# Attention scores with both products over all 128 partition rows, and a mask product in fp32r

## The chip, the cores and the metric

The kernel runs on one core of one Trainium2 chip. The metric is the device time of one execution in microseconds (us), given as the median of several executions. The engines are TensorE (PE; its weight loads stand apart as PEld), VectorE (DVE), ScalarE (ACT), GpSimd (POOL) and SyncE (SP, which issues most loads).

## The reference, cut to what matters

Two layers of a trunk work on 256 latent and 256 context tokens of width 1024. Each layer is a gated feed-forward block, three parallel token mixers, and a second feed-forward block. Mixers A and B are attention with 8 query heads of width 64 in two groups; the four heads of a group share one key and one value head. In the second layer only the latent tokens have queries.

```python
def gqa_softmax(q, k, v, mask, sink):
    kv, g = q.shape[2], q.shape[3]
    s = jnp.einsum('bqkgd,bskd->bkgqs', q, k).astype(jnp.float32) * (q.shape[-1] ** -0.5)
    if mask is not None:
        s = jnp.where(mask, s, -jnp.inf)
    ...
    o = jnp.einsum('bkgqs,bskd->bqkgd', p.astype(v.dtype), v)
```

Mixer A masks latent keys further than 128 positions away; mixer B has no mask. Mixer C is a gated linear memory, whose weights between tokens of one block are masked by the same two triangles.

## The kernel before

All tokens (512 rows, four blocks of 128; blocks 0 and 1 latent, 2 and 3 context) stay on the chip, and weights stream in. To keep fp32 accuracy with the fp32r format, every large product is taken in three parts: high times high, high times low, low times high (`mm3`, lines 194 to 196, the bulk of the work of TensorE). ACT makes the high part of a weight tile (L162), DVE or POOL the low part (L163).

A score of one head needs 64 rows of contraction. The query tile `Q[s]` of group s stacks the high part in one half of the partitions and the low part in the other (`q_cols`, L786 and L787). The key tile `K`, `[P, 3, T]` in fp32r, has at index s the key's high part of group s in both halves, and at index 2 the low parts of the two groups, each in its own half (`k_cols`, L826 to L828). So the first score product (L1012), over 128 rows, gives high times high plus low times high; the second (L1015) runs over the 64 rows of slice `hi`, and adds high times low:

```python
nc.tensor.matmul(ps[:, :nkey], Q[:, c, q], K[:, s, k0:512], start=True, stop=False)
if masked:
    nc.tensor.matmul(ps[:, 0:256], self.identr, ..., start=False, stop=False)
nc.tensor.matmul(ps[:, :nkey], Q[hi, c, q], K[hi, 2, k0:512], start=False, stop=True)
```

Latent queries see 512 keys, context queries 256. For latent queries of mixer A a product of a bf16 identity with a bf16 mask (L1014) adds the mask between the two. An attention step works on two heads: scores, row maximum on DVE (L1017), exponential on ACT (L1027), reciprocal on DVE (L1037), scaling (L1041, L1043); two steps later the transposes of the weights (L1055) and their split into parts (L189, L190), and a step after that the products with the values (L1070, L1072). There are 32 steps in the first layer (64 products of L1015) and 16 in the second (32).

A scheduler of the framework orders each engine's instructions by its own estimates, within priorities that follow the program. Between the attention steps it places other work: the query projections of mixer B and value projection of C (`tok_tasks`), and convolution projections (`conv_task`), all in `mm3`. Each engine then runs its list strictly in that order and waits on semaphores.

The masks are loaded once, by SP, in `more_consts`: `self.mask` in fp32 for mixer C (L1223), `self.maskr` and `self.identr` in bf16 for L1014.

Of the kernel before, what the change touches and what calls it, by code (L numbers as in the profile page):

```python
# [10 lines left out]
F32 = mybir.dt.float32  # L11
F32R = mybir.dt.float32r
# [6 lines left out]
P = 128  # L19
D = 1024  # L20
NK = 8
T = 512
# [44 lines left out]
class Builder:  # L67
# [40 lines left out]
    # ---------------------------------------------------------------- units  # L108
# [78 lines left out]
    # ---------------------------------------------------------------- helpers  # L187
# [17 lines left out]
    def rsqrt(self, ss, n, scale):  # L205
        """ss [P, n] sums of squares -> 1/sqrt(ss*scale + eps)"""
# [3 lines left out]
        # x is minus half the argument, which the seed's constant allows for  # L210
# [12 lines left out]
    # ---------------------------------------------------------------- setup  # L223
# [20 lines left out]
    def more_consts(self):  # L244
# [8 lines left out]
        self.mask = load("mask", [P, 2, P], a["mask"])  # L253
# [4 lines left out]
        self.identr = cp.tile([P, P], BF16, name="identr")  # L258
        nc.vector.tensor_copy(self.identr, self.ident)
        self.maskr = cp.tile([P, 3, P], BF16, name="maskr")  # L260
        for n in range(2):
            nc.vector.tensor_copy(self.maskr[:, 2 * n, :], self.mask[:, n, :])
        nc.vector.memset(self.maskr[:, 1, :], 0.0)
# [41 lines left out]
    # ---------------------------------------------------------------- adaLN  # L305
    def ada_first(self, h):
        """half h of the shift and scale of the first sub-layer"""
# [28 lines left out]
    def ada_tasks(self, l, ms):  # L336
        """blocks ms of the modulation (shift, scale, gate of each sub-layer): products on the vector engine,
        the sum over the partitions on the tensor engine while the next block's products run"""
# [73 lines left out]
    def ada_gate(self, l, k, ps):  # L412
        """the gate rows times the weight of the sub-layer and the gain of its output's norm"""
# [22 lines left out]
    # ---------------------------------------------------------------- norms  # L436
    def prenorm_stat(self, tbs, st):
        """the normalised rows of token blocks"""
# [51 lines left out]
    def post_evac(self, st, ps, tb, n, add):  # L490
        """adds a part of half n of the output of token block tb"""
        y = self.y_half(st, tb, n)
        if add:
            self.nc.vector.tensor_tensor(out=y, in0=ps, in1=y, op=ALU.add)
        else:
            self.copy(y, ps)

    def post(self, st, ps, tbs, n, add):
        """what follows a half of the columns of a sub-layer's output: its sum and, when add is final, its norm"""
# [3 lines left out]
    def closing(self, st, streams, add, keys, mm, done, turn):  # L503
        """the last products of a sub-layer's output and what follows them. keys[n] are the units of half n,
        mm(ps, tb, i, unit) adds the product of the ith; the latent tokens come first, and their chain
        of norms runs beside the products of the others"""
# [45 lines left out]
    def post_half(self, st, tbs, n, last, ds):  # L552
        """square sums and gated copy of half n of the output, which lies in Y or, if ds, in PSUM"""
# [23 lines left out]
    # ---------------------------------------------------------------- FFN  # L577
    def ffn_tasks(self, l, i, k, streams, st, pre, done, turn, halves=None, rest=None):
        """st holds the normalised input, pre(s) brings it for the later streams;
        done(s) is called when the residual of stream s is updated"""  # L580
# [5 lines left out]
        for part, nf in enumerate(FF_PARTS):  # L586
# [41 lines left out]
            def early_half(h, s, n, hs=hs):  # L628
                """half h of the contraction of unit n for the tokens of stream s"""
                def fn(units):  # L630
# [8 lines left out]
                    # one start clears the written bits of the whole bank  # L639
# [56 lines left out]
    # ---------------------------------------------------------------- mixer  # L696
    def tok_tasks(self, l, name, n, kper, tbs, ms, evac):
        """token-major projection of the columns called name, n wide"""
# [25 lines left out]
    def by_stream(self, tasks, pre):  # L724
        """one task of several, the latent tokens first"""
# [11 lines left out]
    def rope(self, dst, src, nh, tb, cos, sin, eng=None, out=None):  # L737
        """dst, src [P, nh*64] (src may be PSUM); rotates pairs of a latent token block"""
# [735 lines left out]
```

## Time and profile before

| what | value |
|---|---|
| median of 3 runs | 2339.59 us (2339.14 to 2345.08) |
| span of the profiled execution | 2339.1 us |
| PE busy | 2243.5 us, 96% |
| DVE busy | 1574.0 us, 67% |
| ACT busy | 1025.0 us, 44% |
| POOL busy | 198.7 us, 8% |
| L1015, second score product | 96 instructions |
| attention of the first layer | 494.7 us to about 690 us |
| attention of the second layer | 1835.7 us to about 1950 us |

The profiled execution has no time of its own beside its span of 2339.1 us, which agrees with the median to 0.5 us. Busy times of PE hold the drain of each product, which lies beside the next product; so the start times in a timeline tell more of PE than its busy share.

### The profile page before, as it was taken

The numbers are of one execution on the slowest core, as the hardware profiler recorded it, in microseconds if no ns is written. First come the engines' busy times: TensorE is split into PE (matmuls) and PEld (weight loads), VectorE is DVE, ScalarE is ACT, GpSimd is POOL, SyncE is SP. The second block draws the span as 40 slices with busy tenths as digits, with TensorE's granted clock in tenths as the row PEclk, the third lists the DMA queues.
The fourth block names the chain that finished last, engine by engine and source line by source line (L and its number), as shares of the span: only waits on it lengthen the run. The fifth ranks groups of instructions, "written<-read, shape, count | busy, mean of one in ns | idle before, by whom it ended". The sixth has DMA issues, their size and how long they took to land.

```text
span 2339.1 us, 30561 instructions
## 1 busy us (share of the span) xinstructions
PE 2243.5 (96%) x11666; PEld 1848.6 (79%) x11666; DVE 1574.0 (67%) x2709; ACT 1025.0 (44%) x1637; POOL 198.7 (8%) x115
## 2 busy tenths in 40 slices
PE   7999999899999999999999989999999899996998
PEld 4877777776678888888878788787878668996997
DVE  3987775788776654664444378778768677867555
ACT  3322222567887433442222253222235488754443
POOL 0000001123410000200000020000012220003001
PEclk9999999999999999999999999999999899998999
DMA  7756563411122224434343327656643103464664
GB/s 274 224 191 184 164 215 103 133 63 38 37 89 75 81 84 135 138 122 135 117 126 117 113 90 221 193 186 192 194 126 118 55 28 118 154 227 143 189 186 144
DMA packets 123523, 322.98 MB, mean 138 GB/s; under 512 B 12392, under 2 KB 25768, under 8 KB 122608
## 3 DMA queue, kind: packets, MB, share of 16 engines
q1 hardware_dynamic: 110224, 309.83, 41.8%
q10 hardware_dynamic: 13152, 11.21, 1.6%
q8 instruction: 91, 1.49, 0.3%
q14 instruction: 56, 0.46, 0.1%
HBM read 316.72 MB, written 4.28 MB: 137 GB/s over the span
## 4 chain that ended last, share of the span: by engine, by line
PE 83%; DVE 11%; ACT 4%; issue 1%; DMA 1%; POOL 0%; ACTq 0%; DVEq 0%
PE ps L194 25%; PE ps L195 25%; PE ps L196 25%; PE ps L1244 1%; PE ps L1015 1%; DVE sm L220 1%; PE ps L1055 1%; DVE lo L163 1%; PE ps L1012 1%; DVE sm L219 1%; PE ps L364 1%; PE ps L1213 1%; DVE slot L574 1%; PE ps L1070 1%; PE ps L466 1%
## 5 line engine op out<-in xcount | busy, mean ns | idle before, releaser
L162 ACT ACTIVATE hi<-raw 128x1024 fp32r<-128x1024 f32 (+1 forms) x444 | 456.0, 1031 | 769.7 <-PE ps L195 261.8
L194 PE MATMUL ps<-slot,hi 128*128 128x512 f32 (+1 forms) x2232 | 777.6, 350 | 7.1 <-ACT slot L189 4.9
L195 PE MATMUL ps<-slot,hi 128*128 128x512 f32 (+1 forms) x2232 | 775.8, 348 | 0.5 <-DVE slot L190 0.4
L196 PE MATMUL ps<-slot,lo 128*128 128x512 f32 (+1 forms) x2232 | 773.3, 347 | 0.0
L163 DVE TENSOR_TENSOR lo<-raw,hi 128x1024 fp32r<-128x1024 f32 (+2 forms) x395 | 475.1, 1205 | 287.6 <-ACT hi L162 285.6
L194 PEld LDWEIGHTS ps<-slot,hi 128*128 128x128 f32 x2232 | 419.6, 189 | 75.6 <-ACT slot L189 7.1
L196 PEld LDWEIGHTS ps<-slot,lo 128*128 128x128 f32 x2232 | 421.1, 189 | 57.5
L195 PEld LDWEIGHTS ps<-slot,hi 128*128 128x128 f32 x2232 | 421.0, 189 | 56.1 <-DVE slot L190 1.4
L194 PE MATMUL ps<-hi,slot 128*128 128x512 f32 (+2 forms) x1048 | 404.4, 386 | 3.0 <-DVE slot L828 1.9
L195 PE MATMUL ps<-lo,slot 128*128 128x512 f32 (+2 forms) x1048 | 402.0, 384 | 4.0 <-DVE lo L163 2.5
L196 PE MATMUL ps<-hi,slot 128*128 128x512 f32 (+2 forms) x1048 | 401.4, 384 | 2.9 <-DVE slot L190 2.9
L356 DVE SCALAR_TENSOR_TENSOR t<-raw,sc,t 128x1024 f32<-128x1024 f32 x224 | 280.4, 1281 | 130.8 <-DMA raw<-in_w_ada_dram 130.6
L194 PEld LDWEIGHTS ps<-hi,slot 128*128 128x128 f32 x1048 | 199.0, 190 | 49.1 <-issue 8.9
L196 PEld LDWEIGHTS ps<-hi,slot 128*128 128x128 f32 x1048 | 198.8, 190 | 44.3 <-DVE slot L190 3.1
L195 PEld LDWEIGHTS ps<-lo,slot 128*128 128x128 f32 x1048 | 199.0, 190 | 43.8 <-DVE lo L163 4.9
L163 POOL TENSOR_TENSOR lo<-raw,hi 128x1024 fp32r<-128x1024 f32 (+1 forms) x49 | 116.8, 2389 | 683.4 <-ACT hi L162 508.8
L189 ACT ACTIVATE slot<-t 128x512 fp32r<-128x512 f32 (+1 forms) x138 | 80.3, 594 | 183.4 <-DVE t L606 158.1
L563 POOL TENSOR_TENSOR slot<-slot,slot 128x512 f32<-128x512 f32 x20 | 30.3, 1524 | 1321.4 <-DMA raw<-in_w_down_dram 733.3
L606 DVE TENSOR_TENSOR t<-ps,t 128x512 f32<-128x512 f32 (+1 forms) x88 | 54.7, 622 | 87.9 <-PE ps L196 86.7
L190 DVE TENSOR_TENSOR slot<-t,slot 128x512 fp32r<-128x512 f32 (+1 forms) x138 | 88.6, 651 | 6.9 <-ACT slot L189 6.5
L1017 DVE TENSOR_REDUCE sm<-ps 128x1 f32<-128x512 f32 (+1 forms) x96 | 55.9, 593 | 13.1 <-PE ps L1015 12.6
L466 PE MATMUL ps<-ident,t 128*128 128x128 f32 x176 | 30.5, 331 | 34.4 <-DVE t L449 33.4
(194 smaller groups left out, 1911.3 us busy)
## 6 DMA issues: line engine op xcount, KB each, us to landing
raw<-in_w_gu_dram SPq DMA_DIRECT2D x176, 512.0 KB
raw<-in_w_ada_dram SPq DMA_DIRECT2D x128, 512.0 KB
raw<-in_w_down_dram SPq DMA_DIRECT2D x92, 512.0 KB
raw<-in_w_fm_dram SPq DMA_DIRECT2D x64, 512.0 KB
raw<-in_w_br_dram SPq DMA_DIRECT2D x24, 512.0 KB
raw<-in_w_out_dram SPq DMA_DIRECT2D x24, 512.0 KB
slot<-in_w_ada_dram SPq DMA_DIRECT2D x16, 512.0 KB
raw<-in_w_down_dram SPq DMA_DIRECT2D x20, 256.0 KB
```

What stands on the lines that cost most here:

```text
L162: self.nc.scalar.activation(out=hi, in_=raw, func=AF.Copy)
L163: eng.tensor_tensor(out=lo, in0=raw, in1=hi.bitcast(F32), op=ALU.subtract)
L189: self.nc.scalar.activation(out=hi, in_=src, func=AF.Copy)
L190: self.nc.vector.tensor_tensor(out=lo, in0=src, in1=hi.bitcast(F32), op=ALU.subtract)
L194: mm(out, lh, rh, start=start, stop=False, **kw)
L195: mm(out, lh, rl, start=False, stop=False, **kw)
L196: mm(out, ll, rh, start=False, stop=stop, **kw)
L356: v.scalar_tensor_tensor(out=acc, in0=units[0], scalar=c, in1=acc, op0=ALU.mult, op1=ALU.add)
L466: nc.tensor.transpose(pt[:, o:o + P], xn[b][:, c * P:(c + 1) * P], self.ident)
L563: eng.tensor_tensor(out=self.y_half(st, tb, n), in0=src[q], in1=self.Gt[tb // 2][:, n * 512:(n + 1) * 512], op=ALU.mult)
L606: nc.vector.tensor_tensor(out=hid[:, :W], in0=ps[:, :W], in1=hid[:, :W], op=ALU.mult)
L1017: v.tensor_reduce(out=mx[:, :1], in_=ps[:, :nkey], axis=AX.X, op=ALU.max)
```

## The change

The key tile grows to `[P, 4, T]`: index 2 + s now holds the low part of group s in both halves of the partitions, for which `k_cols` makes one more copy on DVE for each group (two for each mixer, four for each layer, eight in all). The second score product runs over all 128 rows; its lower-order half now multiplies the query's low part with the key's low part, a term that was left out before. The identity and the mask for L1014 are kept in fp32r, and mixer C reads the same mask tile; the fp32 mask is now loaded into a temporary tile of the rotating pool `t512`, at the same place in SP's list. All else in the diff is comments and blank lines. In the changed file the lines behind the mask load stand one number higher (L1012 is L1013, L828 is L829, the new copy is L830).

```diff
         self.anti = load("anti", [P, P], a["anti"])
-        self.mask = load("mask", [P, 2, P], a["mask"])
+        mask = self.t512([P, 2, P])
+        nc.sync.dma_start(mask, a["mask"])
...
-        self.identr = cp.tile([P, P], BF16, name="identr")
+        self.identr = cp.tile([P, P], F32R, name="identr")
...
-        self.maskr = cp.tile([P, 3, P], BF16, name="maskr")
+        self.maskr = cp.tile([P, 3, P], F32R, name="maskr")
...
-            K = self.slot([P, 3, T], F32R)
+            K = self.slot([P, 4, T], F32R)
...
-                nc.vector.tensor_tensor(out=K[a, 2, :], in0=pt[a], in1=K[a, g, :].bitcast(F32), op=ALU.subtract)
+                nc.vector.tensor_tensor(out=K[a, 2 + g, :], in0=pt[a], in1=K[a, g, :].bitcast(F32), op=ALU.subtract)
+                nc.vector.tensor_copy(K[b, 2 + g, :], K[a, 2 + g, :])
...
-            hi = slice(64 * s, 64 * s + 64)
...
-                nc.tensor.matmul(ps[:, :nkey], Q[hi, c, q], K[hi, 2, k0:512], start=False, stop=True)
+                nc.tensor.matmul(ps[:, :nkey], Q[:, c, q], K[:, 2 + s, k0:512], start=False, stop=True)
...
-                        v.tensor_tensor(out=Wt[:, n, :], in0=src, in1=self.mask[:, dr, :], op=ALU.add)
+                        v.tensor_tensor(out=Wt[:, n, :], in0=src, in1=self.maskr[:, 2 * dr, :].bitcast(F32), op=ALU.add)
```

With the diff the scheduler places some instructions elsewhere. On PE, at the first scores of the first layer, there stood before (ps are PSUM tiles, hi and lo a weight tile's parts, slot the key, query or token tiles):

```order
L194 MATMUL ps_3807<-hi_3695,slot_3112 128x512
L195 MATMUL ps_3807<-lo_3696,slot_3112 128x512
L1012 MATMUL ps_3837<-slot_3739,slot_3763 128x512
L1014 LDWEIGHTS identr
L1014 MATMUL ps_3837<-maskr,identr 128x256
L1015 MATMUL ps_3837<-slot_3739,slot_3763 128x512
```

At the same place of PE's list stands now:

```order
L195 MATMUL ps_3811<-lo_3696,slot_3112 128x512
L196 MATMUL ps_3811<-hi_3695,slot_3114 128x512
L194 MATMUL ps_3811<-hi_3695,slot_3112 128x512
L195 MATMUL ps_3811<-lo_3696,slot_3112 128x512
L1013 MATMUL ps_3841<-slot_3739,slot_3767 128x512
L1015 MATMUL ps_3841<-maskr,identr 128x256
L1016 MATMUL ps_3841<-slot_3739,slot_3767 128x512
```

Three more projection products (L196, L194, L195) stand ahead of the first score, and the separate weight load of the identity is gone from the list.

On DVE, where the second layer's keys and queries are split ahead of its first scores, there stood before (slot_14529 and slot_14541 are the keys of mixers A and B, slot_14553 and slot_14554 the queries of the two groups):

```order
L827 COPY slot_14529<-slot_14529 64x512
L828 TENSOR_TENSOR slot_14529<-ps_14530,slot_14529 64x512
L827 COPY slot_14541<-slot_14541 64x512
L828 TENSOR_TENSOR slot_14541<-ps_14542,slot_14541 64x512
L787 TENSOR_TENSOR slot_14553<-ps_14555,slot_14553 64x4x128
L787 TENSOR_TENSOR slot_14553<-ps_14564,slot_14553 64x4x128
L787 TENSOR_TENSOR slot_14554<-ps_14555,slot_14554 64x4x128
L1017 TENSOR_REDUCE sm_14579<-ps_14575 128x1
```

There stands now on DVE (keys slot_14533 and slot_14547, queries slot_14561):

```order
L828 COPY slot_14547<-slot_14547 64x512
L830 COPY slot_14533<-slot_14533 64x512
L829 TENSOR_TENSOR slot_14547<-ps_14548,slot_14547 64x512
L828 COPY slot_14533<-slot_14533 64x512
L829 TENSOR_TENSOR slot_14533<-ps_14534,slot_14533 64x512
L830 COPY slot_14547<-slot_14547 64x512
L830 COPY slot_14533<-slot_14533 64x512
L828 COPY slot_14547<-slot_14547 64x512
L829 TENSOR_TENSOR slot_14547<-ps_14548,slot_14547 64x512
L788 TENSOR_TENSOR slot_14561<-ps_14563,slot_14561 64x4x128
L830 COPY slot_14547<-slot_14547 64x512
L788 TENSOR_TENSOR slot_14561<-ps_14572,slot_14561 64x4x128
```

Three of the four new copies stand ahead of the first split of the queries (L787 before, L788 now), the fourth right behind it.

On PE, at the first scores of the second layer, there stood before:

```order
L196 MATMUL ps_14515<-hi_14451,slot_13827 128x512
L194 MATMUL ps_14522<-hi_14451,slot_13825 128x512
L195 MATMUL ps_14522<-lo_14452,slot_13825 128x512
L1012 MATMUL ps_14575<-slot_14529,slot_14553 128x512
L1014 LDWEIGHTS identr
```

There stands now on PE (hi_14455 is hi_14451 of before):

```order
L194 MATMUL ps_14526<-hi_14455,slot_13829 128x512
L195 MATMUL ps_14526<-lo_14456,slot_13829 128x512
L196 MATMUL ps_14526<-hi_14455,slot_13831 128x512
L194 MATMUL ps_14526<-hi_14455,slot_13829 128x512
L195 MATMUL ps_14526<-lo_14456,slot_13829 128x512
L196 MATMUL ps_14526<-hi_14455,slot_13831 128x512
L194 MATMUL ps_14505<-hi_14499,slot_13830 128x512
L1013 MATMUL ps_14583<-slot_14533,slot_14561 128x512
```

Five projection products that stood behind the first scores stand ahead of them now.

## Rows read from the trace of the kernel before

**Rows 1.** The profile page: TensorE's share, and the chain that ended last, by engine

```profile
PE 2243.5 (96%) x11666; PEld 1848.6 (79%) x11666; DVE 1574.0 (67%) x2709; ACT 1025.0 (44%) x1637; POOL 198.7 (8%) x115
PE 83%; DVE 11%; ACT 4%; issue 1%; DMA 1%; POOL 0%; ACTq 0%; DVEq 0%
```

**Rows 2.** Timeline of PE, unmasked scores, 512 keys: start, duration, instruction

```profile
1936.18 0.39 PE L196 MATMUL ps<-slot,lo 128*128 128x512 f32 x1
1936.41 0.40 PE L1012 MATMUL ps<-slot,slot 128*128 128x512 f32 x1
1936.74 0.49 PE L1015 MATMUL ps<-slot,slot 64*128 64x512 f32 x1
1937.16 0.51 PE L1012 MATMUL ps<-slot,slot 128*128 128x512 f32 x1
1937.59 0.50 PE L1015 MATMUL ps<-slot,slot 64*128 64x512 f32 x1
1938.02 0.33 PE L1055 MATMUL ps<-ident,t 128*128 128x128 f32 x1
```

**Rows 3.** Timeline of PE, masked scores of the first layer

```profile
496.05 0.40 PE L1012 MATMUL ps<-slot,slot 128*128 128x512 f32 x1
496.28 0.28 PE L1014 MATMUL ps<-maskr,identr 128*128 128x256 bf16 x1
496.50 0.50 PE L1015 MATMUL ps<-slot,slot 64*128 64x512 f32 x1
496.93 0.49 PE L1012 MATMUL ps<-slot,slot 128*128 128x512 f32 x1
```

**Rows 4.** Timeline of PE, scores of context queries, 256 keys

```profile
553.45 0.28 PE L1012 MATMUL ps<-slot,slot 128*128 128x256 f32 x1
553.66 0.38 PE L1015 MATMUL ps<-slot,slot 64*128 64x256 f32 x1
553.97 0.38 PE L1012 MATMUL ps<-slot,slot 128*128 128x256 f32 x1
```

**Rows 5.** Timeline of PE, masked scores of the second layer, at half clock

```profile
1848.56 0.63 PE L1012 MATMUL ps<-slot,slot 128*128 128x512 f32 x1
1848.99 0.44 PE L1014 MATMUL ps<-maskr,identr 128*128 128x256 bf16 x1
1849.36 0.79 PE L1015 MATMUL ps<-slot,slot 64*128 64x512 f32 x1
1850.08 0.80 PE L194 MATMUL ps<-hi,slot 128*128 128x512 f32 x1
1850.68 0.60 PE L195 MATMUL ps<-lo,slot 128*128 128x512 f32 x1
```

**Rows 6.** The chain that ended last, by line: 494 to 700, then 1834 to 1960

```profile
by line: PE ps L196 12.3%; PE ps L194 12.2%; PE ps L195 12.1%; PE ps L1015 6.9%; PE ps L1055 6.4%; PE ps L1012 4.9%; PE ps L1070 3.7%; PE ps L1072 3.6%; ACT t L1027 3.3%; DVE sm L1017 2.8%; DVE t L190 2.6%; DVE slot L960 2.5%; DVE sm L1024 
by line: PE ps L1015 12.0%; PE ps L194 11.9%; PE ps L196 11.5%; PE ps L195 10.9%; PE ps L1055 10.7%; PE ps L1012 9.7%; PE ps L1070 5.9%; PE ps L1072 5.3%; DVE sm L1017 2.2%; PE ps L1014 2.1%; ACT t L1027 1.8%; DVE sm L1033 1.7%; PE ps L1136 
```

**Rows 7.** Busy time by 25-us window: PE, PEld, DVE, ACT, POOL, granted clock

```profile
545.00:570.00 25.00, 22.39 (x121) 17.44 (x121) 20.01 (x71) 15.13 (x38) 10.22 (x9) 0.93 0.15 46
620.00:645.00 25.00, 23.60 (x127) 17.69 (x126) 17.22 (x39) 22.50 (x41) 11.04 (x7) 1.00 0.08 24
1885.00:1910.00 25.00, 23.26 (x136) 17.61 (x135) 21.14 (x53) 20.51 (x44) 3.18 (x3) 0.86 0.01 2
1910.00:1935.00 25.00, 25.00 (x158) 20.34 (x158) 18.93 (x48) 24.18 (x45) 13.97 (x8) 1.00 0.20 64
```

**Rows 8.** The same windows for L1015 alone: PE, PEld, clock

```profile
620.00:645.00 25.00, 4.48 (x10) 1.83 (x10) 1.00 0.08 24
1835.00:1860.00 25.00, 4.75 (x6) 1.71 (x6) 0.68 0.07 22
1910.00:1935.00 25.00, 3.95 (x8) 1.46 (x8) 1.00 0.20 64
```

**Rows 9.** Line L827, the copy of the keys' high parts: nanoseconds min/median/max

```profile
L827 DVE CAST slot<-slot x8: 421/422/2282, 485.6 to 1833.7; 64x512 fp32r<-64x512 f32 x8
```

**Rows 10.** Timeline: first scores of the second layer

```profile
1835.73 0.77 PE L1012 MATMUL ps<-slot,slot 128*128 128x512 f32 x1 [8.41 <-DVE slot L787]
```

More of the change, by code (lines that the diff above doesn't have):

```diff
@@ L257, in more_consts @@
         nc.vector.memset(self.ones, 1.0)
-        self.identr = cp.tile([P, P], BF16, name="identr")
+        self.identr = cp.tile([P, P], F32R, name="identr")
         nc.vector.tensor_copy(self.identr, self.ident)
-        self.maskr = cp.tile([P, 3, P], BF16, name="maskr")
+        self.maskr = cp.tile([P, 3, P], F32R, name="maskr")
         for n in range(2):
-            nc.vector.tensor_copy(self.maskr[:, 2 * n, :], self.mask[:, n, :])
-        nc.vector.memset(self.maskr[:, 1, :], 0.0)
+            nc.vector.tensor_copy(self.maskr[:, 2 * n, :], mask[:, n, :])
+        nc.vector.memset(self.maskr[:, 1, :].bitcast(F32), 0.0)
     def load_layer(self, name, shape, src, bufs=1):
```

## The prediction

> **What bounds the kernel now.** I read the page first, then the chain of waits, then timelines of TensorE in the two attention stages, since the change touches nothing else of weight. TensorE is busy for 96% of the span, and the chain that ended last runs on it for 83% [rows 1]: time taken out of TensorE's list counts, as long as nothing else is late. The timelines show what the busy share hides: how long one product holds up the next. Read the start times, not the durations. In a plain stream a product over 512 columns starts 0.23 us after the one before (1936.18 to 1936.41) [rows 2]. Around the half-row product L1015 the stream breaks up: L1012, ahead of it, holds the engine for 0.33 us instead of 0.23, L1015 itself for 0.42, and the L1012 behind it, which stands ahead of another L1015 as well, for 0.43 [rows 2]. So one L1015 costs 0.10 us ahead of itself, 0.19 in itself, and 0.10 behind itself: 0.39 us over a full-row product of the same columns. The other forms say the same. With 256 keys L1012 takes 0.21 and L1015 0.31 [rows 4], where 0.12 would be half of 0.23: again 0.09 and 0.19. With a mask ahead, the L1014 of 256 columns takes 0.22 instead of 0.12, and L1015 0.43 [rows 3]; the L1012 in front of L1014 keeps its 0.23, so the bf16 mask product itself disturbs nothing. At half clock, where L1012 takes 0.43, L1014 takes 0.37, L1015 0.72 and the L194 behind it 0.60 [rows 5]: 0.16 (over half of 0.43) and 0.29 and 0.17, in all 0.62.
>
> **The change part by part.**
>
> *Second product over all rows.* L1015 becomes a product of the same shape as L1012 and the streams around it, so I take the whole 0.39 us (0.62 at half clock) as gone. Six products lie in the cold stretch 1835 to 1860 [rows 8]; I price those six cold and the other 90 warm. In the first layer that is 64 x 0.39 = 25.0 us of TensorE's time, in the second 26 x 0.39 + 6 x 0.62 = 13.9, together 38.9.
>
> Not all of it lies on the path. In the window from 494 to 700, 206 us long, L1015 has 6.9% of the chain, 14.2 us [rows 6]. All 64 hold the engine for 32 x 0.42 + 32 x 0.31 = 23.4 us (half of them have 512 keys, half 256). So 61% lie on the path; the rest pass while TensorE would have waited for DVE or ACT anyway. From 1834 to 1960, 126 us, L1015 has 12.0%, 15.1 us [rows 6], of 26 x 0.42 + 6 x 0.72 = 15.2: practically all. On the path the saving is 25.0 x 0.61 + 13.9 = 29.2 us.
>
> *What is late next.* The softmax on DVE and ACT must now keep up with a faster TensorE. From 620 to 645 ACT is busy for 22.50 of 25 us [rows 7], which leaves 2.5 us, and 10 products there [rows 8] would save 3.9: 1.4 too much. From 1910 to 1935 ACT has 24.18 [rows 7], which leaves 0.8, and 8 products [rows 8] would save 3.1: 2.3 too much. That is 3.7 us that engines without idle time cannot give. Engines that run their lists in order never use all their idle time, so I double it: 7.4 us taken back, an estimate from these rows. Its bounds are 0 (lists fit as well as now) and all 29.2.
>
> *Eight more copies on DVE.* The nearest row is L827, the same copy of the high parts: 0.42 us, once 2.28 [rows 9]. The order shows three copies ahead of the first split of queries that the first score waits for, in the second layer and likewise in the first: 3 x 0.45 with the gaps = 1.35 us later. What covers it: five projection products are moved ahead of the scores in the second layer, 5 x 0.23 = 1.15 us, three in the first, 0.69 us. Loss 0.2 + 0.7 = 0.9 us. Behind the waiting score stand TensorE's whole list and the softmax; in the second layer TensorE already waits 8.41 us there [rows 10]. With a copy of 2.28 in each place the loss would be about 2 us more for each copy that is hit; without any cover 2.7 us; without any effect 0.
>
> *Mask in fp32r, mask load.* A 256-column product in fp32r is what L1012 with 256 keys is, and half of 0.23 us is what L1014 takes now without the disturbance of L1015; the separate load of the identity joins the stream. I take 0, with 32 x 0.1 = 3.2 us as the upper bound if the identity's load is not hidden. The mask's load keeps its place in SP's list, so no weight comes later. Mixer C reads another tile of the same shape and takes the same time. The added low-times-low term costs nothing: a product's columns decide its place in the stream, not its rows.
>
> *Sum.* 2339.1 - 29.2 + 7.4 + 0.9 = 2318.2 us. The profiled span is within 0.5 us of the median, so I forecast 2318.5 us.
>
> *A rule against it.* The start times say that a full-row product hides the weight load of the next one, since only 0.23 us pass between starts [rows 2]. The Trainium skill, "TensorE: Matmul & The Clock Gate", Part 3, under what overlaps and what doesn't, says that a weight load overlaps running products only when the row group differs. By that rule a product over 128 rows would hold up its neighbours as one over 64 does, and the sum would be 2339 instead of 2318; the stream of this kernel disagrees with it.
>
> **The rivals.**
>
> *Full effect, 2301 (2299 to 2309).* DVE and ACT follow: all 38.9 us, less 0.9 for the copies. For it: from 1910 to 1935 TensorE has no idle time at all though ACT is busy for 24.18 of 25 us [rows 7], so a nearly full neighbour need not stall it. Against: 39% of the first layer's saving is off the chain now.
>
> *The softmax takes it all, 2337 (2332.6 to 2339).* The waits of TensorE grow by as much as the products shrink. For it: from 545 to 570 TensorE is busy for 22.39 of 25 us, DVE for 20.01 [rows 7], so TensorE waits already where no product is slow. Against: in the second layer L1015 is almost wholly on the chain [rows 6], and there at least 13.9 - 2 x 2.3 = 9 us should show; to lose that too the lists must fit much worse.
>
> *The stall stays, 2339.* The price belongs to what the second product does, loading new weights and adding into a bank that was just written, and not to its 64 rows; then the weight load of a full-row second product is not hidden either, and 96 products stall as before. Against: `mm3` adds three products with new weights into one bank, 0.23 us apart [rows 2]. The rule of the Trainium skill above (same page, Part 3) would end here.
>
> *The clock falls more often, 2350.* TensorE waits more, and the granted clock drops to 1.2 GHz after waits. It does so now: 0.93 from 545 to 570 and 0.86 from 1885 to 1910, windows in which TensorE was idle for 2.6 and 1.7 us [rows 7], and 0.68 around the wait of 8.41 us [rows 8, 10]. A mean of 0.86 means 28% of 25 us at half clock, 7 us, which cost 3.5. The two stages have some twelve windows of 25 us; if the nine that keep the full clock fell as far, that is 32 us against the 21 saved: 2350. It decides from six such windows on. Against: from 620 to 645 TensorE idles 1.4 us and keeps 1.00 [rows 7].
>
> **How the numbers follow.** A measurement of this kernel can tell about 0.3%, 7 us, from no change: 2332.6 and 2346.6. Chances: my forecast, a partial gain from 2309 to 2332.6, 0.67; full effect 0.13; softmax takes it all 0.10; the stall stays 0.04; slower by the clock 0.06. Faster is 0.67 + 0.13 = 0.80, same 0.14, slower 0.06. The range reaches down into the full effect, to 2302, and up just into the swallowed case, to 2334; about 0.05 lie below and 0.15 to 0.2 above.
>
> **What would show it.** Right: second products start 0.23 us (0.12 with 256 keys) before their successor, and L1012 ahead of them too; L1014 in fp32r about 0.12; first scores in the second layer wait some 9 us for the query split; TensorE's waits for DVE and ACT between 494 and 700 grow by several us, and L1015's share of the chain falls under half. Wrong: starts still 0.42 apart; cold windows inside the attention stages; L1014 at 0.2 us; or differences outside the two attention stages, where I expect the same distances as before.

## The result, and the profile of the changed kernel

The changed kernel takes 2327.83 us (median of 4 runs, 2321.42 to 2328.41), the kernel before 2339.36 us in the same comparison (4 runs, 2337.81 to 2345.08). The ratio is 0.9944, with an interval from 0.9931 to 0.9956: faster by 11.5 us. The forecast was 2318.5 us with a range from 2302 to 2334. The profiled execution of the changed kernel is the fastest of its four (2321.42 us, span 2319.6), so it stands 19.5 us under the profiled span of before: more than the medians differ by, and the text below says where that comes from. One run of all those below, of e10, took 2751.70 us at a mean granted clock of 0.75 and is left out of its median. Lines stand one number higher than before: L1013 is the first product, L1015 the mask, L1016 the second product.

The page, in the form of [rows 1]:

```profile
PE 2207.9 (95%) x11666; PEld 1844.3 (80%) x11666; DVE 1572.1 (68%) x2717; ACT 1023.0 (44%) x1637; POOL 198.1 (9%) x115
PE 80%; DVE 11%; ACT 6%; issue 2%; DMA 1%; POOL 0%; ACTq 0%; DVEq 0%; POOLq 0%
```

As many matmuls as before (11666) keep TensorE busy for 35.6 us less, yet the span falls by 19.5 only; ACT's share of the chain has grown from 4% to 6%.

The timeline of PE where unmasked scores of the second layer run, which answers to [rows 2]:

```profile
1909.10 0.40 PE L1013 MATMUL ps<-slot,slot 128*128 128x512 f32 x1
1909.34 0.39 PE L1016 MATMUL ps<-slot,slot 128*128 128x512 f32 x1
1909.57 0.40 PE L1013 MATMUL ps<-slot,slot 128*128 128x512 f32 x1
1909.81 0.40 PE L1016 MATMUL ps<-slot,slot 128*128 128x512 f32 x1
1910.04 0.60 PE L1056 MATMUL ps<-ident,t 128*128 128x128 f32 x4
```

Read the start times again: 0.24, 0.23, 0.24, 0.23 us, where [rows 2] had 0.33, 0.42, 0.43, 0.43. The second product has become one more piece of the plain stream. With 256 keys it is the same (compare [rows 4]): 0.11 and 0.12 us from start to start.

```profile
553.53 0.28 PE L1013 MATMUL ps<-slot,slot 128*128 128x256 f32 x1
553.64 0.28 PE L1016 MATMUL ps<-slot,slot 128*128 128x256 f32 x1
553.76 0.28 PE L1013 MATMUL ps<-slot,slot 128*128 128x256 f32 x1
```

The first scores of the second layer, the place of [rows 10], and masked scores a little later:

```profile
1830.80 0.76 PE L1013 MATMUL ps<-slot,slot 128*128 128x512 f32 x1 [8.35 <-DVE slot L788]
1831.36 0.41 PE L1015 MATMUL ps<-maskr,identr 128*128 128x256 f32 x1
1831.58 0.63 PE L1016 MATMUL ps<-slot,slot 128*128 128x512 f32 x1
1832.00 0.63 PE L1013 MATMUL ps<-slot,slot 128*128 128x512 f32 x1
...
1834.89 0.39 PE L194 MATMUL ps<-hi,slot 128*128 128x512 f32 x1
1835.12 0.39 PE L195 MATMUL ps<-lo,slot 128*128 128x512 f32 x1
1835.35 0.39 PE L196 MATMUL ps<-hi,slot 128*128 128x512 f32 x1
1835.58 0.40 PE L1013 MATMUL ps<-slot,slot 128*128 128x512 f32 x1
1835.82 0.28 PE L1015 MATMUL ps<-maskr,identr 128*128 128x256 f32 x1
1835.93 0.39 PE L1016 MATMUL ps<-slot,slot 128*128 128x512 f32 x1
1836.16 0.39 PE L194 MATMUL ps<-hi,slot 128*128 128x512 f32 x1
```

The wait for the query split is still there, 8.35 us. The fp32r mask takes 0.11 us at full clock. The engine starts at half clock (0.42 us for the second product), and is back at full clock 4 us later, while [rows 5] still shows half clock 13 us behind the first score.

To see where the time went, one view of each kernel: busy time in the two attention stages, each from its first score to its last (PE, PEld, DVE, ACT, POOL, then the granted clock, DMA share and GB/s). The kernel before:

```profile
494.70:675.30 180.60, 172.90 (x877) 127.08 (x877) 141.90 (x367) 135.37 (x291) 55.70 (x36) 0.99 0.14 43
1835.70:1937.20 101.50, 96.54 (x512) 69.78 (x512) 72.90 (x178) 73.66 (x149) 25.17 (x13) 0.89 0.10 32
```

The changed kernel:

```profile
495.10:669.00 173.90, 154.87 (x876) 125.47 (x875) 140.25 (x367) 134.32 (x293) 55.90 (x36) 0.98 0.14 44
1830.80:1918.20 87.40, 79.08 (x506) 66.75 (x507) 69.58 (x179) 72.34 (x148) 25.18 (x13) 0.98 0.11 37
```

Three things are to be read here. TensorE's busy time falls by 18.0 us in the first layer and by 17.5 in the second. Its idle time (length less busy) grows from 7.7 to 19.0 us and from 5.0 to 8.3: 14.6 us together. And the granted clock of the second layer rises from 0.89 to 0.98: of 101.5 us some 11.2 were lost to half clock (0.11 x 101.5), now 1.7 of 87.4; in the first layer it goes the other way, 1.8 to 3.5. The same arithmetic gives each stage a length at full clock, its length times its clock: 178.8 and 90.3 us before, 170.4 and 85.7 after. It is an estimate, since it takes TensorE for the limit wherever the clock was halved. Outside the two stages the kernels take 2057.0 and 2058.3 us, nearly the same, as the prediction expected.

What TensorE waits for in the first layer's attention of the changed kernel (487 to 693, the four longest rows; line that waits, what it waits for, us in total, times, longest):

```profile
PE ps L1071 <- ACT t L1028: 4.5, 2, 3.4
PE ps L1056 <- ACT t L1028: 2.6, 4, 0.8
PE ps L194 <- DVE slot L829: 2.6, 1, 2.6
PE ps L1071 <- ACT t L189: 2.1, 2, 1.9
```

L1071 is a product with the values, L1056 the transpose of the weights, L1028 the exponential on ACT. The two rows that end with L1028 have 7.1 us, where the longest rows of before were 2.3 us (L1055 for DVE's L1020), 1.4 and 1.1. (The 2.6 us of L194 for L829 stand ahead of the first score, and were 1.9 before.) By the program neither product reads the exponential that ended its wait: L1071 multiplies the split weights of an earlier step, L1056 reads weights that were scaled after their exponential. Both write into one of the kernel's eight PSUM tiles, and an exponential, once it has read its scores, frees one; that they wait for the tile is read from the program, since the trace does not name it.

The longest of these waits can be followed back. The chain that ended last (the first three lines), then the timeline:

```profile
524.92 1.35 DVE slot L1144 x4
526.27 1.11 DVE slot L1146
528.17 1.21 DVE slot L1155
530.89 0.20 DVE L1021 TENSOR_SCALAR sm<-sm,nsink 128x1 f32<-128x1 f32 x1
531.12 0.69 ACT L1028 ACTIVATE t<-ps,sm 128x512 f32<-128x512 f32 x1 [3.31 <-DVE sm L1021]
531.96 0.58 PE L1071 MATMUL ps<-t,slot 128*128 128x256 f32 x1 [3.40 <-ACT t L1028]
```

ACT had been idle for 3.31 us as well. What both waited for is VectorE: between the row maximum (L1018, at 524.33) and its scaling (L1021) its list holds the scans and gates of mixer C, lines 1144 to 1155, for 6 us. The kernel before has the same scans at the same place and reaches the same product 37.1 us behind its first score, the changed kernel 36.9, with the longer wait:

```profile
525.42 1.74 DVE slot L1143 x4
531.84 0.39 PE L1070 MATMUL ps<-t,slot 128*128 128x256 f32 x1 [0.71 <-ACT t L1027]
```

So nearly all that the first layer's products had saved up to 532 us was lost again at this one place: a wait of 3.40 us (3.38 in e1 and in e3) instead of 0.71, 2.7 of the 11.3 us by which the first layer's idle time grew. Behind that wait, from 530.90 to 537.70, the granted clock is 0.50, which by the estimate above costs another 3.4 us.

In the second layer, a stretch of the changed kernel in the form of [rows 7]:

```profile
1890.00:1915.00 25.00, 24.08 (x176) 21.87 (x175) 20.18 (x52) 24.84 (x47) 14.94 (x8) 1.00 0.17 55
```

ACT is busy for 24.84 of 25 us and TensorE, for 24.08, almost as much: two full engines.

### The profile page after: what moved, and what is told of

Its sections match the earlier page's. It is cut to its first block, busy times and chain, and to the rows that moved or that the text cites. A ratio compares the mean times of both kernels' runs of the same rounds, so it can differ in the third digit from the quotient of the medians.

```text
span 2319.6 us, 30573 instructions
## 1 busy us (share of the span) xinstructions
PE 2207.9 (95%) x11666; PEld 1844.3 (80%) x11666; DVE 1572.1 (68%) x2717; ACT 1023.0 (44%) x1637; POOL 198.1 (9%) x115
## 4 chain that ended last, share of the span: by engine, by line
PE 80%; DVE 11%; ACT 6%; issue 2%; DMA 1%; POOL 0%; ACTq 0%; DVEq 0%; POOLq 0%
PE ps L194 25%; PE ps L195 24%; PE ps L196 24%; PE ps L1245 1%; DVE sm L220 1%; ACT t L1028 1%; DVE lo L163 1%; ACT hi L162 1%; DVE slot L575 1%; PE ps L365 1%; DVE sm L219 1%; PE ps L1214 1%; PE ps L467 1%; DMA slot<-in_w_ada_dram 1%; ACT t L1042 1%
## 5 line engine op out<-in xcount | busy, mean ns | idle before, releaser
L194 PE MATMUL ps<-slot,hi 128*128 128x512 f32 (+1 forms) x2232 | 777.8, 350 | 6.6 <-ACT slot L189 4.9
L195 PE MATMUL ps<-slot,hi 128*128 128x512 f32 (+1 forms) x2232 | 775.5, 348 | 0.5 <-DVE slot L190 0.3
L196 PE MATMUL ps<-slot,lo 128*128 128x512 f32 (+1 forms) x2232 | 773.1, 347 | 0.0
L194 PEld LDWEIGHTS ps<-slot,hi 128*128 128x128 f32 x2232 | 419.4, 189 | 75.3 <-ACT slot L189 6.2
L196 PEld LDWEIGHTS ps<-slot,lo 128*128 128x128 f32 x2232 | 420.6, 189 | 57.8
L195 PEld LDWEIGHTS ps<-slot,hi 128*128 128x128 f32 x2232 | 420.5, 189 | 56.3 <-DVE slot L190 1.4
L194 PE MATMUL ps<-hi,slot 128*128 128x512 f32 (+2 forms) x1048 | 402.5, 384 | 4.1 <-DVE slot L829 2.6
L195 PE MATMUL ps<-lo,slot 128*128 128x512 f32 (+2 forms) x1048 | 400.5, 382 | 4.1 <-DVE lo L163 4.1
L196 PE MATMUL ps<-hi,slot 128*128 128x512 f32 (+2 forms) x1048 | 400.4, 383 | 2.9 <-DVE slot L190 2.9
L194 PEld LDWEIGHTS ps<-hi,slot 128*128 128x128 f32 x1048 | 198.7, 190 | 48.7 <-issue 8.1
L195 PEld LDWEIGHTS ps<-lo,slot 128*128 128x128 f32 x1048 | 198.5, 189 | 43.1 <-DVE lo L163 5.0
L196 PEld LDWEIGHTS ps<-hi,slot 128*128 128x128 f32 x1048 | 198.2, 189 | 42.9 <-DVE slot L190 3.2
L190 DVE TENSOR_TENSOR slot<-t,slot 128x512 fp32r<-128x512 f32 (+1 forms) x138 | 88.7, 652 | 5.8 <-ACT slot L189 5.3
L1018 DVE TENSOR_REDUCE sm<-ps 128x1 f32<-128x512 f32 (+1 forms) x96 | 55.2, 591 | 8.1 <-PE ps L1016 7.7
```

Of the source, the lines that this page charges most:

```text
L190: self.nc.vector.tensor_tensor(out=lo, in0=src, in1=hi.bitcast(F32), op=ALU.subtract)
L194: mm(out, lh, rh, start=start, stop=False, **kw)
L195: mm(out, lh, rl, start=False, stop=False, **kw)
L196: mm(out, ll, rh, start=False, stop=stop, **kw)
L1018: v.tensor_reduce(out=mx[:, :1], in_=ps[:, :nkey], axis=AX.X, op=ALU.max)
```

## The experiments

Each ratio is to the kernel before on the same chip, whose medians were 2340.35 us (17 runs) for e1 to e4, 2340.65 (19) for e6, e7, e9 and e10, and 2339.67 (17) for e5, e8, e11 and e12. "At full clock" is always a stage's length times its granted clock, from one profile.

**Rows alone (e1_full_rows).** Before, with the four-row key tile, the copies and the full-row product, and the mask left in bf16:

```diff
-            K = self.slot([P, 3, T], F32R)
+            K = self.slot([P, 4, T], F32R)
...
+                nc.vector.tensor_copy(K[b, 2 + g, :], K[a, 2 + g, :])
...
-                nc.tensor.matmul(ps[:, :nkey], Q[hi, c, q], K[hi, 2, k0:512], start=False, stop=True)
+                nc.tensor.matmul(ps[:, :nkey], Q[:, c, q], K[:, 2 + s, k0:512], start=False, stop=True)
```

> Second product over all rows with the eight copies, mask and identity still in bf16. Theory A (the gain comes from the second product's rows): the time of the whole change, 2322 to 2329 us; second products 0.23 us (0.12 with 256 keys) before their successor. Theory B (the gain comes from the mask product in fp32r): 2337 to 2341 us.

Measured: 2324.96 us (6 runs), ratio 0.9939 (0.9924 to 0.9953). The whole gain is here.

**Mask alone (e2_mask_fp32r).** Before, with identity and mask in fp32r and the mask loaded into a temporary tile:

```diff
-        self.identr = cp.tile([P, P], BF16, name="identr")
+        self.identr = cp.tile([P, P], F32R, name="identr")
...
-        self.maskr = cp.tile([P, 3, P], BF16, name="maskr")
+        self.maskr = cp.tile([P, 3, P], F32R, name="maskr")
```

> Mask and identity in fp32r and the mask loaded into a temporary tile, second product still over 64 rows. Theory A: no change, 2336 to 2342 us, second products still 0.42 us before their successor. Theory B: 2322 to 2329 us.

Measured: 2339.7 us (12 runs), ratio 1.0001 (0.9991 to 1.0011). The mask's type is worth nothing either way.

**The changed kernel once more (e3_after_again).** No edit; it ran on the same chip as e1, e2 and e4.

> The changed kernel once more, unedited, for a second profile. Its four runs were one of 2321.4 (the profiled one) and three near 2328. Theory C (TensorE's clock differs between runs): 2321 to 2329 us, and a profile that is longer than 2319.6 us of span has more half-clock time in the attention stages, about 12 us more for 6 us of time (say 20 us instead of 10.2 in the second layer). Theory D (waits on transfers or engines differ): the same half-clock stretches to 1 us, and 6 us more of waits elsewhere.

Measured: 2324.76 us (6 runs), ratio 0.9939 (0.9925 to 0.9953). Its profile (span 2325.4) shows how far two executions of one kernel differ:

```profile
496.50:674.90 178.40, 158.12 (x875) 128.03 (x874) 140.48 (x367) 134.27 (x293) 55.89 (x36) 0.96 0.14 43
1836.20:1923.60 87.40, 79.03 (x506) 66.70 (x507) 69.52 (x179) 72.25 (x148) 25.17 (x13) 0.98 0.12 37
```

The second layer repeats to 0.1 us. The first is 4.5 us longer than in the profile above, at a clock of 0.96 instead of 0.98; at full clock it is 171.3, as against 170.4. So a large part of the 5.8 us between the two spans is clock, and it fell in the first layer.

**Keys of mixer A ahead of the queries, those of B behind (e4_keys_a_first).** The changed kernel with the order of the preparing steps changed (`k_cols` takes one mixer at a time):

```diff
-        out += vm_[:nv] + one(self.k_cols) + qcols(0) + qb[:QC]
+        out += vm_[:nv] + one(lambda R: self.k_cols(R, 0)) + qcols(0) + one(lambda R: self.k_cols(R, 1)) + qb[:QC]
```

> The changed kernel with the program order keys of mixer A, queries of mixer A, keys of mixer B. DVE then splits the queries after two new copies and without the keys of B ahead. Theory E (the wait ahead of the second layer's first score and the half clock behind it cost 5 to 10 us): that wait falls from 8.4 to about 5 us, the half-clock stretch shrinks, 2317 to 2325 us. Theory F (the softmax is late anyway): within 2 us of the changed kernel, about 2327 us.

Measured: 2321.87 us (6 runs), ratio 0.9925 (0.991 to 0.9941), 2.9 us under e3 with intervals that overlap. The time lies in Theory E's range, but the wait of the second layer's first score only fell to 8.01 us: E's mechanism did not show.

**Without the scaling of the weights (e6_no_scale_before, e7_no_scale_after).** The same edit in both kernels:

```diff
-            for e in range(2):
-                t = E[i][e]
-                if x == 0 or e == 0:
-                    nc.scalar.activation(out=t[:, :nkey], in_=t[:, :nkey], func=AF.Copy, scale=r[:, e:e + 1])
-                else:
-                    nc.gpsimd.tensor_scalar(out=t[:, :nkey], in0=t[:, :nkey], scalar1=r[:, e:e + 1], scalar2=None,
-                                            op0=ALU.mult)
```

> The kernel before, with the scaling of the attention weights by the reciprocal of their sum left out (ACT loses 176 instructions of 0.45 to 0.65 us in the attention stages, POOL 16), so that the softmax has slack. Theory G (the softmax on ACT and DVE takes back most of the first layer's saving): the second score products stay as they are, and the gap to its partner with full rows is 20 us or more. Theory H (it is the copies and the clock): the gap is that of the unedited kernels, 12 to 17 us.

> The changed kernel with the same scaling left out. Theory G: 20 us or more under its partner, and from its first score to its last score the first layer gains 12 us or more where the unedited pair gained 6.6. Theory H: 12 to 17 us under its partner, first layer as in the unedited pair.

Measured: 2349.87 us (4 runs), ratio 1.0043 (1.0027 to 1.006), for the kernel before; 2325.78 (4), ratio 0.9943 (0.9928 to 0.9957), for the changed one. Less work made the kernel before slower: its first layer ran at a clock of 0.94 (0.99 without the edit), 11.6 us lost instead of 1.8. So the 24 us between the two, though over the 20 that Theory G named, are not the softmax alone. The first layer's stage of e6, then both stages of e7:

```profile
494.40:687.50 193.10, 181.13 (x878) 133.88 (x878) 144.37 (x367) 110.25 (x244) 36.77 (x21) 0.94 0.14 42
497.30:670.80 173.50, 156.47 (x876) 128.36 (x875) 139.55 (x366) 110.60 (x246) 36.76 (x21) 0.96 0.15 47
1833.10:1921.90 88.80, 79.96 (x506) 68.43 (x507) 70.27 (x179) 60.23 (x126) 14.27 (x6) 0.95 0.12 39
```

In the changed kernel ACT does 24 us less in the first layer and 12 less in the second, and at full clock the stages shrink by 4 (166.6 beside 170.4) and 1 us (84.4 beside 85.7). TensorE still idles 17.0 and 8.8 us. At full clock the first layer of the pair differs by 14.9 us (181.5 less 166.6), where the unedited pair has 8.4: Theory G's sign, but 2.7 of these 6.5 us are that the kernel before became longer, which no slack on ACT explains. What is left for G is the 4 us; ACT's load as such holds back little, and products still wait for single exponentials (L1028).

**The half-row product twice (e8_half_twice).** Before, with one more line:

```diff
+                nc.tensor.matmul(ps[:, :nkey], Q[hi, c, q], K[hi, 2, k0:512], start=False, stop=False)
```

> The kernel before, with the half-row second product issued twice in succession (the small product of high queries and low keys is added twice). Theory P: the price is paid where the stream changes between 128 and 64 rows. Then the first of the two starts about 0.23 us before the second (512 keys; 0.12 with 256), and only the second holds its full-row successor off for 0.42 (0.31); the time grows by some 14 us (64 products, 32 x 0.23 + 32 x 0.12 + 32 x 0.23 = 18.6 us, about three quarters of it on the path). Rival Q: every half-row product pays for itself; then 0.42 lie between the two as well, and the time grows by some 28 us.

Measured: 2360.58 us (one run), 20.9 us over the kernel before, between P's 14 and Q's 28. Timeline of PE, unmasked scores (L1015 and L1016 are the two):

```profile
1955.92 0.40 PE L1012 MATMUL ps<-slot,slot 128*128 128x512 f32 x1
1956.24 0.49 PE L1015 MATMUL ps<-slot,slot 64*128 64x512 f32 x1
1956.58 0.39 PE L1016 MATMUL ps<-slot,slot 64*128 64x512 f32 x1
1956.90 0.49 PE L1012 MATMUL ps<-slot,slot 128*128 128x512 f32 x1
1957.33 0.49 PE L1015 MATMUL ps<-slot,slot 64*128 64x512 f32 x1
```

The two take 0.34 and 0.32 us, 0.66 together, where one alone takes 0.42 [rows 2]: the second adds 0.24, the price of a plain product, and L1012 ahead and behind keep their 0.32 and 0.43. Theory P's sum (0.65) holds, Q's (0.84) doesn't, though P had put the whole price on the second of the two, and it is divided over both: about half on the way in, half on the way out. (Both load the same weights; a pair with two sets of weights was not tried.) The span grew by 19.7 us; 10.3 of these stand in the stages at full clock (183.5 and 95.9 us); the rest is about what the lower clock of the stages costs (0.95 and 0.88 instead of 0.99 and 0.89: 9.8 us).

**Spare products ahead of the second layer's scores (e9_before_warm, e10_after_warm).** In both kernels 40 products over 128 rows into a tile that nobody reads:

```diff
+        def warm(_):
+            ps = self.psum()
+            for i in range(40):
+                nc.tensor.matmul(ps, ms["hi"][0][:, 0, :P], ms["hi"][0][:, 0, :], start=i == 0, stop=i == 39)
...
+            out.append(([], warm))
```

> The kernel before with 40 spare full-row products (9.3 us of TensorE's time, results unused) in the wait ahead of the second layer's first score. Theory J (the half clock behind that wait costs time, and half-row products prolong it): no half-clock stretch of 20.5 us there, time 5 to 10 us less than before, although it does more. Theory K (the clock matters little): 2339 us or some us more.

> The changed kernel with the same 40 spare products. Theory J: its half-clock stretch of 10.2 us goes, 2 to 5 us less than the changed kernel; so the gap to the kernel before with spare products falls to some 8 to 12 us. Theory K: about 2325 us or some us more.

Measured: 2341.09 us (10 runs), ratio 1.0004 (0.9995 to 1.0014), and 2337.29 (9), ratio 0.9985 (0.9976 to 0.9995). Neither kernel gained, so Theory J's times both failed. The spare products came behind the wait, not into it (timeline of PE, kernel before with the edit):

```profile
1833.91 10.85 PE L924 MATMUL ps<-slot 128*128 128x512 f32 x40 [8.17 <-DVE slot L828]
```

The first score starts 8.9 us later (1844.6 instead of 1835.7), yet the last only 0.5 us later (1937.7 instead of 1937.2), since the stage ran at 0.96 instead of 0.89 (windows of the same kernel):

```profile
1844.60:1937.70 93.10, 91.31 (x520) 68.56 (x518) 68.16 (x175) 72.89 (x147) 25.20 (x13) 0.96 0.11 35
```

The kernel before wins back through its clock what it lost; the changed kernel had nothing to win there (its stage ran at 0.94, 85.1 us at full clock) and loses some 11 us (0.9985 beside e3's 0.9939). With that, the distance between the two falls to 3.8 us, though at full clock their stages still differ by 7.5 and 4.3: here the changed kernel has the lower clock in both (0.96 and 0.94 beside 0.99 and 0.96).

**Copies taken off DVE (e5_zeros_pool).** The changed kernel with zeros in place of the copies, so that the low-times-low term is left out:

```diff
-                nc.vector.tensor_copy(K[b, 2 + g, :], K[a, 2 + g, :])
+                nc.gpsimd.memset(K[b, 2 + g, :].bitcast(F32), 0.0)
```

> The changed kernel, with the four copies of the key's low parts in each layer replaced by zeros that GpSimd writes: the second product adds over 128 rows the same terms as in the kernel before (the low-times-low term is left out). The prediction put 0.9 us on the copies. If that price is right, the wait of the second layer's first score falls from 8.35 us by about 1 us and the time by 0 to 2 us (2322 to 2327 beside the changed kernel's own 2324 to 2328). Rival: the copies ran in a gap of VectorE, so that wait and time stay within 0.3 us and 2 us. A rival on the other side: the writes on GpSimd come late, and the wait grows.

Measured: 2324.63 us (5 runs), ratio 0.9933 (0.9922 to 0.9945). No gain that can be told. The wait grew (9.19 us instead of 8.35), but it says nothing of the copies, since the lists differ: with the copies gone, the five projection products stand behind the first score again, as in the kernel before. VectorE's own list says more. From the second layer's first key copy to the first split of the queries it takes 4.64 us before (1830.26 to 1834.90) and in e5 (1822.75 to 1827.39), and 5.76 in the changed kernel:

```profile
1824.21 0.42 DVE L828 CAST slot<-slot 64x512 fp32r<-64x512 f32 x1
1829.97 0.68 DVE L788 TENSOR_TENSOR slot<-ps,slot 64x512 fp32r<-64x512 f32 x1
```

So the copies do stand in the way, by 1.12 us, and the five products that moved ahead of the score cover them.

**A shorter list on DVE ahead of the scores (e11_gates_later, e12_gates_later_before).** The order of e4, and the gate chain made to depend on the query split by a copy of one column, in both kernels:

```diff
+            v.tensor_copy(g[:, 0, 0:1], R["q0"][1][:, 0, 0:1].bitcast(F32))
```

> The changed kernel with a reordered VectorE list in front of the scores: key copies of the first half, the query split, then key copies of the second half, and the second layer's gate chain (L1107 to L1126) held back until the query split is done. Theory E: what the second layer's first score waits 8.35 us for is VectorE's list; then the wait falls to 3 to 5 us, the half-clock stretch behind it (10.2 us) becomes shorter or goes, and the time falls by 3 to 9 us under the changed kernel, 2316 to 2323. Rival: the gates are needed early, the 5 us of gate work turn up in front of the first gated products instead, and the time stays at 2324 to 2328.

> The kernel before with the same reordered VectorE list. Theory C: more than half of the second layer's gain came from the clock, since half-row products prolong a half-clock stretch that the wait of 8.41 us starts. Then, if the wait falls to 3 to 5 us and the stretch of 20.5 us goes with it, this kernel gains 8 to 14 us, more than the changed one does, and their distance shrinks from 13 us to 4 to 8. Rival: the gain of the change is in the products alone; then the distance stays at 12 to 15 us.

Measured: 2323.12 us (5 runs), ratio 0.9928 (0.9916 to 0.994), and 2337.82 (12), ratio 0.999 (0.9978 to 1.0003). The wait did fall, to 3.09 us in the changed kernel and 2.48 in the other. The changed kernel with the edit (timeline, then a row of the waits from 1819 to 1941):

```profile
1825.83 0.77 PE L1013 MATMUL ps<-slot,slot 128*128 128x512 f32 x1 [3.09 <-DVE slot L829]
```

```profile
PE ps L1071 <- DVE t L190: 2.6, 1, 2.6
```

The first score comes 5.0 us earlier (1825.8), the last 0.8 us later (1919.0 instead of 1918.2): the lead is lost within the stage. Part of it is seen in the new wait of 2.6 us for a split by DVE (L190), whose list now holds the gates at 1832 to 1842; the clock of the stage was 0.95. Theory E had the cause of the wait right and its worth wrong: 2323.12 us stands at the upper end of its range, and the intervals of e11 and e3 overlap. In e12 the half clock only came later, 0.66 from 1855 to 1880, and the stage took 109.1 us. The distance between the two is 14.7 us, the rival's number: a shorter wait did not take the clock's part out of the comparison.

## Why the prediction was right, and what of it was mis-sized

**The half-row product's price.** The starts of 0.42 us are gone, the second product's share of the chain falls from 12.0% [rows 6] to 3.1% (L1016 in the row below, from 1829 to 1941), and e1 and e2 show that the rows alone do it. Where the price comes from is shown by e8: it is paid at the change between 64 and 128 rows, once in and once out. The Trainium skill, "TensorEngine Tiling (Array Packing)", Key Properties, says that a change of tiling mode makes the engine drain; the pair, 0.24 us dearer than a single one, agrees. The rival by the Trainium skill, "TensorE: Matmul & The Clock Gate", Part 3, under which full rows stall as well, is refuted by 0.23 us between starts.

```profile
by line: PE ps L195 8.4%; ACT t L1028 8.4%; PE ps L194 8.3%; PE ps L196 8.3%; ACT t L1042 5.2%; ACT t L189 5.1%; DVE sm L1018 4.0%; PE ps L1013 4.0%; PE ps L1071 3.6%; PE ps L1056 3.5%; issue 3.5%; PE ps L1073 3.1%; PE ps L1016 3.1%; DVE sl
```

The prediction named [rows 2] for three products of `mm3` that are 0.23 us apart; those rows hold one of them. The three stand in the changed kernel's timeline above, at 1834.89, 1835.12 and 1835.35.

**The size of it** is the term that was off. The prediction took 0.39 us for each of 96 products, 38.9 us of TensorE's time (25.0 and 13.9). Busy time fell by 18.0 and 17.5; taking out the clock's part (1.7 more lost in the first layer, 9.5 fewer in the second) leaves 19.7 and 8.0, 27.7 us. By the start times of the 96 second products and their neighbours in both traces, idle time left out and half-clock stretches counted half, it is 21.6 and 10.3, or 0.33 for each. A part of the difference is plain: the 0.10 us "behind itself" was read from 512-column successors, but 33 of the 96 stand ahead of a transpose L1055, which starts its own successor 0.165 us later instead of 0.109 (medians): 0.06. The rest was not taken apart.

**What lies off the path, and what is late next.** The prediction let 9.7 us fall off the path (39% of 25.0) and gave 7.4 us back to the softmax, 17.1 together. TensorE's idle time in the two stages grew by 14.6 us, 11.3 in the first layer, 5.3 of these in waits that an exponential ended (8.2 us now, 2.9 before). The sum of the two steps came out nearly right; the doubling of 3.7 was a choice, and that it fits is luck, since the mechanism was another. The prediction read the limit from how full ACT is. But e7 takes a sixth of ACT's load away and gains 4 and 1 us at full clock, and at the longest wait ACT itself was idle for 3.31 us: the row maximum's scaling stood in VectorE's list behind 6 us of mixer C's scans and gates. That accounts for 2.7 us of the growth; the other waits, each under 2 us, were not taken apart. No run takes the scans out of the list, but where they end at another time the wait follows: L1021 starts at 528.90 in e5, 530.89 in the changed kernel and 533.84 in e11, and TensorE waits 1.41, 3.40 and 4.36 us.

**Copies and mask.** 0.9 us for the copies. In the second layer the terms came out: 1.12 us on VectorE where 1.35 were taken, covered by the five products, and a wait of 8.35 us as against 8.41. The total of the copies cannot be told from nothing by the time of e5. For the mask 0 was taken, and 1.0001 measured (e2).

**The clock.** The prediction had it only as a rival that makes the kernel slower. In the second layer it went the other way. The products alone, at full clock, give 8.4 and 4.6 us between the two profiles, 13.0 us, where the forecast's terms make 20.9. The clock of the stages gives 9.5 less 1.7, so 7.8 more; the sum of 20.8 us agrees with the 19.5 of the spans, and that the forecast's 20.9 is so near is partly luck. This profile is a lucky one, too: in e1 and e3 the first layer's clock is 0.96, not 0.98, so that 7.1 us are lost there instead of 1.8. To that extent the rival's mechanism fits the first layer, where TensorE waits more; the clock's part is then 9.5 less 5.3, or 4.2 us. The runs agree. Each run has its mean granted clock; the runs of the kernel before beside the experiments and of the changed kernel (the first comparison and e3), sorted by it, at the three clocks that both kernels have:

| mean clock of the run | before: mean us (runs) | changed: mean us (runs) | difference |
|---|---|---|---|
| 0.981 | 2340.1 (10) | 2328.3 (2) | 11.8 |
| 0.982 | 2337.6 (9) | 2327.3 (4) | 10.3 |
| 0.983 | 2336.6 (3) | 2323.7 (1) | 12.9 |
| all runs | 2340.4 (53, clock 0.9805) | 2325.7 (10, clock 0.9825) | 14.7 |

At the same clock the change is worth 10 to 13 us, and 2 to 4 us more come because the changed kernel runs at a higher mean clock. The profiles say the same: at full clock before, e2 and e9 have 178.8, 177.6, 178.8 and 90.3, 89.7, 89.4 us in the two stages; after, e1, e3 and e10 have 170.4, 171.4, 171.3, 171.3 and 85.7, 85.8, 85.7, 85.1: 7.3 and 4.2 us, 11.5 together.

So the range held and the side was right; the forecast of 2318.5 was too low by 9 us because the half-row products were priced 7 to 11 us too high (31.9 or 27.7 us for 38.9), and the clock made good a part of it.

No edit tried here beats the changed kernel beyond its interval; e4 (0.9925) and e11 (0.9928) come nearest.

## What to carry to other kernels

Read what a matmul costs from start to start, and read its neighbours too: here a 64-row product in a 128-row stream cost more in its neighbours and in itself than its own columns, and filling the array with rows that add a harmless term was free on TensorE. A wait that ends with one engine can have its cause on another: follow it back until an engine was busy all the way. Price such a stall for each kind of successor apart before multiplying, and count separately what TensorE will then wait for. When two profiles of kernels with long waits are compared, multiply each stage's length by its granted clock first; otherwise a run's clock is taken for an effect of the edit.

## What the runs showed of the hardware that was not expected

Half-row products go with a longer half-clock stretch behind the same wait of about 8.4 us. In the 25 us from the second layer's first score the granted clock is 0.69 before and 0.71 in e2, but 0.92 in the changed kernel, in e1 and in e3. Spare full-row products ahead of the scores raised it to 1.00 (e9). Why was not tried.

A product can change its neighbour's recorded start without changing the sum. In e1 the bf16 mask stands between full-row products:

```profile
1840.12 0.39 PE L1012 MATMUL ps<-slot,slot 128*128 128x512 f32 x1
1840.35 0.28 PE L1014 MATMUL ps<-maskr,identr 128*128 128x256 bf16 x1
1840.39 0.48 PE L1015 MATMUL ps<-slot,slot 128*128 128x512 f32 x1
1840.71 0.39 PE L194 MATMUL ps<-hi,slot 128*128 128x512 f32 x1
```

The mask seems to take 0.04 us and its successor 0.32, but from L1012 to L194 it is 0.59 us, beside 0.58 with the fp32r mask above (1835.58 to 1836.16): one start alone would have told a gain that isn't there.
